# One row of reciprocal sums: two POOL transfers become one from ScalarE, and its transpose moves behind half a product

## The chip, the cores and the metric

The kernel runs on one core of a Trainium2 chip. The metric is the device time in microseconds of one execution. A core has a matrix engine (TensorE, in the profile PE, with its weight loads as PEld), a vector engine (VectorE, DVE), a scalar engine (ScalarE, ACT), GpSimd (POOL) and SyncE (SP), which here only issues transfers. Each engine works through its own list of instructions in order; semaphores tie the lists together. Transfers (DMAs) can be issued by SP, ACT and POOL, and all are carried out by the same 16 DMA engines.

## The reference

One layer with a state-space branch, an attention branch, a gated merge and an output projection, for 1024 positions and width 1024. What matters here is the attention, with 16 heads of width 64:

```python
fcum = jnp.cumsum(log_f, axis=-1)
for blk in range(seqlen // ATT_BLOCK):                       # blocks of 128 queries
    s = jnp.einsum('bhqd,bhkd->bhqk', q[:, :, q0:q1], k[:, :, :q1]) * scale
    s = s + fcum[:, :, q0:q1, None] - fcum[:, :, None, :q1]
    s = jnp.where(kpos[None, :] <= qpos[:, None], s, -jnp.inf)
    prob = jax.nn.softmax(s, axis=-1)
    outs.append(jnp.einsum('bhqk,bhkd->bhqd', prob, v[:, :, :q1]))
...
y_att = o * jax.nn.silu(z_att)
```

The softmax divides each query's weighted sum by the sum of its exponentials. In the kernel this division comes last: the weighted sum is formed without it, and is then multiplied by one over the sum. That reciprocal is the number whose way through the chip is changed here.

## The kernel before

**Stages.** The kernel has a prologue (norm, transposes), a state-space stage, an attention stage (about 669 to 1140 us of the profiled execution) and a tail with the last projections. Through all of them runs a `stream` of dense products for the projections, each split into a high and a low part and built as Strassen-like combinations of blocks. One step of the stream is a product of four 128-blocks by three part combinations, 12 matmuls of 128x128 by 512 columns; it is emitted as two halves of 6 matmuls (`Stream.half`), and after each half the stream may also emit loads, splits of operands and small chores. `fill(m, part)` emits as many halves as the plan gives to that place, so that TensorE has work while the attention's softmax passes through DVE and ACT.

**The attention loop.** Heads are worked in 8 pairs (`hp`), each pair in 6 visits (`g`), 48 visits `m = 6 hp + g` in all. A visit handles two blocks of 128 queries against one half (512) of the keys. Its parts, in the order in which they are emitted:

1. `scores`: four tiles of scores in PSUM (tag `s`, four banks); DVE adds the decay and takes the row minimum (line 1526, `ex`, `nm`), ACT takes the exponential with its row sum (line 1530, `ex`, `sm`).
2. `out` for the group of queries finished two visits ago: DVE multiplies by the reciprocals (`rb`, lines 1485 and 1491), and the outputs go on to DRAM from POOL (`ya_dram`, line 1581).
3. `weighted`: the weighted sums of the previous visit (`av`), with TensorE.
4. For the group finished in the previous visit: `free` (DVE, line 1479: weighted sum times gate, out of PSUM) and `send` (line 1446).
5. `settle` (the joint maximum of the two key halves), then `fill(m, 0)`.
6. `scale` (DVE: the reciprocals, tile `ns`, lines 1435 to 1444), loads for later visits on SP, `turned` (TensorE transposes the exponentials into PSUM tiles `pt`, DVE and ACT copy them out as `p`), and `take` (line 1456) for the group that was sent in this visit.
7. `fill(m, 1)`.

A group of queries ends with every second visit, three per pair of heads, 24 in all, and `send` and `take` run in the visits with even `m` after that.

**The row of reciprocals.** `ns` holds one number per query: 128 partitions (queries of a block) by 8 (two key halves or two block pairs `h`, two heads `e`, two blocks `t`). The outputs have the queries along the free axis, so the numbers must become a row and be spread over the 64 partitions of each head. `send` transposes `ns` with TensorE into a PSUM tile `tp` of 8 partitions by 128 (one of the four `s` banks), ACT copies it to a tile `st` (8x128, one of four buffers of the tag `th`, which the gates, the reloads and `rb` share), and POOL writes it to DRAM in two transfers, for `h = 0` and `h = 1`, so that DRAM holds it as `[e][h t c]`. `take` reads it back on SP into `rb`, 64 partitions times, one transfer for each head, 512 numbers in a row.

**What sets the order.** Instructions marked with `pin`, and all of TensorE's, stay in the order in which they are emitted. The others are put into each engine's list by a scheduler that simulates the program; `tc.high_priority()` puts an instruction ahead of the ones without it. The copy `st` has high priority; the POOL transfers are pinned.

Of the kernel before, what the change touches and what calls it, by code (L numbers as in the profile page):

```python
# [8 lines left out]
F32 = mybir.dt.float32  # L9
# [7 lines left out]
P = 128  # L17
T = 1024
D = 1024
NK = D // P  # L20
KH = NK // 2
NT = T // P
HALF = 512
# [63 lines left out]
def hybrid_layer(ctx: ExitStack, tc, a, out):  # L87

    nc = tc.nc
# [17 lines left out]
    nc.vector.memset(eps4, 4.0 * EPS)  # L107

    f_dram = tc.dram_tile([HEADS, T], F32, name="f_dram")
    st_dram = tc.dram_tile([NK, 3, 2, HALF], F32, name="st_dram")  # L110
    r_dram = tc.dram_tile([NG, T], F32, name="r_dram")
    rr_dram = tc.dram_tile([NG, T], F32, name="rr_dram")
    cs_dram = tc.dram_tile([HEADS, T], F32, name="cs_dram")
# [18 lines left out]
    def turn(out_, in_, idn=ident):  # L132
        return tc.keep_in_program_order(nc.tensor.transpose(out_, in_, idn))  # L133

    def pin(op):
        return tc.keep_in_program_order(op)

    def small(name="th"):
        return gp.tile([P, HALF], F32, tag="th", name=name)
# [185 lines left out]
    class Pair:  # L325
# [101 lines left out]
        def do(self, which):  # L427
            if which in (2, 4, 3) or which in (5, 7) and self.sums:
                unit, ch = {2: (0, 0), 4: (1, 0), 3: (0, 1)}.get(which, (1, 1))
                for begin in self.handlers[unit][2:]:  # L430
                    begin(ch)
            if which == 1:
                pool, tag = self.bank
                self.b = pool.tile([P, HALF], F32, tag=tag, bufs=1, name="pb")
                yield from self.matmuls(self.b, 1, "b11", True)
                self.k1 = self.keep(self.b)
            elif which == 2:
                pool, tag = self.other
                ps = pool.tile([P, HALF], F32, tag=tag, bufs=1, name="p" + tag)
                yield from self.matmuls(ps, 2, "b21", True)  # L440
                self.give(0, 0, ps, self.k1, "sum")
            elif which == 6:
                yield from self.matmuls(self.b, 6, "-t2", False)
                self.k2 = self.keep(self.b)
            elif which in (5, 7):
                if which == 5:
                    self.c = pj.tile([P, HALF], F32, tag="c", bufs=1, name="pc")
                    yield from self.matmuls(self.c, 5, "t1", True)
                else:
                    yield from self.matmuls(self.b, 7, "t3", False)  # L450
                    self.k7 = self.keep(self.b)
                self.sums += 1
                if self.sums == 2:
                    self.give(1, 1, self.c, self.k7, "less")
            elif which == 4:
                yield from self.matmuls(self.b, 4, "t4", False)
                (self.closing or (lambda ps: self.give(1, 0, ps)))(self.b)
            elif which == 3:
                yield from self.matmuls(self.c, 3, "-b22", False)
                self.give(0, 1, self.c, self.k2, "from")  # L460
# [26 lines left out]
    class Stream:  # L487
# [61 lines left out]
        def begin(self):  # L549
            self.load_next()  # L550
            self.load_next()
            for p, which in self.steps[:3]:
                self.prepare(p, which)
# [639 lines left out]
    with tc.tile_pool(name="pro", bufs=1, reuse_waits="tile", side="right") as pro, tc.tile_pool(  # L1193
        name="prop", bufs=1, space=PSUM, reuse_waits="tile", side="right"
# [6 lines left out]
        part = pro.tile([P, 1], F32, name="part")  # L1201
# [36 lines left out]
        def turned(tiles, k):  # L1238
            pt = prop.tile([P, HALF], F32, tag="pt", bufs=3, name="pt")
            for j in range(4):  # L1240
                turn(pt[:, j * P : (j + 1) * P], tiles[j][:, k * P : (k + 1) * P]) 
            return pt
# [10 lines left out]
        stream = Stream(order + late + ends, len(order) + 1, len(order) + len(late) + 4)  # L1253
# [57 lines left out]
    with tc.tile_pool(name="ssm", bufs=1, reuse_waits="tile", side="right") as sp, tc.tile_pool(  # L1311
        name="ssmp", bufs=1, space=PSUM, reuse_waits="tile", side="right"
# [42 lines left out]
    with tc.tile_pool(name="att", bufs=1, reuse_waits="tile", side="right") as ap, tc.tile_pool(  # L1355
        name="attp", bufs=1, space=PSUM, reuse_waits="tile", side="right"
    ) as pp:
        rows = [slice(64 * e, 64 * e + 64) for e in range(2)]
# [42 lines left out]
        class Heads:  # L1401
# [44 lines left out]
            def send(self, n):  # L1446

                tp = pp.tile([P, HALF], F32, tag="s", bufs=4, name="tp")
                turn(tp[0:8, 0:P], self.ns[n].rearrange("p h e t -> p (h e t)"))
                st = small("st")[0:8, 0:P]  # L1450
                with tc.high_priority():
                    nc.scalar.activation(st, tp[0:8, 0:P], AF.Copy)
                for h in range(2):
                    pin(nc.gpsimd.dma_start(st_dram[self.hp, n, :, 256 * h : 256 * h + 256], st[4 * h : 4 * h + 4, :]))

            def take(self, n):

                rb = self.rb[n] = small("rb")
                for e in range(2):
                    nc.sync.dma_start(rb[rows[e], :], st_dram[self.hp, n, e : e + 1, :].to_broadcast([64, HALF]))  # L1460

            def load_gates(self, n):

# [34 lines left out]
        def scores(hp, g, u):  # L1498

            pair, h = GROUPS[g]  # L1500
            i = pair[u]
            w = min(HALF, (i + 1) * P - h * HALF)
            s = [pp.tile([P, HALF], F32, tag="s", bufs=4, name="s") for e in range(2)]
            t, keys = q[hp, pair], k[hp, h]
            isl = slice(i % 2 * P, i % 2 * P + P)
            ops = [(t[:, x, isl], keys[:, y, 0:w]) for x, y in ((0, 0), (0, 1), (1, 0))]
            diagonal = h == i // 4
            for m, (x, y) in enumerate(ops):
                for e in range(2):
                    mm(  # L1510
                        s[e][:, 0:w], x[rows[e]], y[rows[e]], start=(m == 0), stop=(m == 2 and not diagonal),
                        skip_group_check=True,
                    )
            if diagonal:
                for n, (x, y) in enumerate(corner):
                    for e in range(2):
                        mm(
                            s[e][:, w - P : w], x[rows[e]], y[rows[e]], start=False, stop=(n == 1),
                            skip_group_check=True,
                        )  # L1520
            hd = heads[hp]
            for e in range(2):
                o = ex[:, e, u, 0:w]
                nm = hd.at(hd.nm, i, h, e)
                pin(
                    nc.vector.tensor_tensor_reduce(  # L1526
                        o, s[e][:, 0:w], fb[hp, h][:, e, 0:w], 1.0, 3.0e38, ALU.add, ALU.min, nm
                    )
                )
                pin(nc.scalar.activation(o, o, AF.Exp, scale=-1.0, bias=nm, accum_out=hd.at(hd.sm, i, h, e)))  # L1530
# [108 lines left out]
        def end(m):  # L1639

            hp, g = divmod(m, 6)
            if 0 <= hp < NK and g % 2:
                yield heads[hp], g // 2
# [12 lines left out]
        rooms = [(0.8, 0.35), (0.8, 0.35), (0.55, 0.25), (0.8, 0.35), (0.75, 0.35), (0.5, 0.25)]  # L1656
        left = [sum(map(sum, rooms)) * sum(weights)]

        def fill(m, part):
            share = weights[min(m // 6, NK - 1)] * rooms[m % 6][part]  # L1660
            to = stream.steps.index((ends[4], 6))
            stream.halves(round((2 * (to - stream.at) - (stream.run is not None)) * share / left[0]))
            left[0] -= share

        made = []
        for m in range(6 * NK + 1):

            stream.visit = m + 1
            hp, g = divmod(m, 6)
            if not g and hp < NK:  # L1670
                heads[hp] = Heads(hp)
            if m < 6 * NK:
                for u in range(2):
                    scores(hp, g, u)
            for hd, which in end(m - 2):
                hd.out(which)
            for one in made:
                weighted(*one)
            for hd, which in end(m - 1):
                hd.free(which)  # L1680
                if m < 6 * NK:
                    hd.send(which)
            stream.release()
            if m == 6 * NK:
                heads[NK - 1].out(2)
                stream.visit = 0
                break
            for hd, which in end(m):
                hd.settle(which)
            fill(m, 0)  # L1690

            for hd, which in end(m):
                hd.scale(which)
                hd.load_gates(which)
            loads(m)
            made = turned(hp, g)
            for hd, which in end(m - 1):
                hd.take(which)
            if m == 6 * NK - 1:
                heads[hp].send(2)  # L1700
            stream.hold()
            fill(m, 1)
            if m == 6 * NK - 1:
                heads[hp].take(2)
# [59 lines left out]
```

## Time and profile before

| | |
|---|---|
| three runs | 1291.77, 1297.4 and 1297.5 us, median 1297.4 us |
| profiled execution, its own time | 1294.79 us |
| its span in the trace | 1293.1 us (1.7 us lie around it) |
| granted TensorE clock | 0.997 |
| busy share of the span | PE 97%, DVE 78%, ACT 61%, POOL 22% |
| sends | 24 transposes `tp`, 24 copies `st`, 48 POOL transfers, 48 SP reads `rb` |

A row of a group reads: line, engine, operation, output<-inputs, shapes, count, then busy time in us, mean ns of one, then the engine's idle time just before these instructions and what ended it. In the timeline a row is start, duration, engine, line, operation, and in brackets the idle time before it. `SPq`, `ACTq` mean the engine's list of issues, not the transfer itself; the time "to landing" runs from the issue to the semaphore that tells of its end.

### The profile page before, as it was taken

The page shows a single profiled execution, that of the slowest core. Times are in us where ns is not written, and L with a number is a line of the kernel's source. Part 1 is how long each engine was busy: PE and PEld are TensorE (multiplying, and loading weights), DVE is VectorE, ACT ScalarE, POOL GpSimd, SP SyncE. Part 2 cuts the span into 40 slices and gives each one's busy share as a digit, 9 for nine tenths or more (in the row PEclk, how much of TensorE's full clock was granted, in tenths as well). Part 3 has the DMA queues.
Part 4 walks back from the last instruction along what each step waited for, and adds up shares of the span by engine and source line. Part 5 has one row for each costly group of instructions (what it writes and reads, how often), then busy time and mean ns, then how long its engine had stood idle before and what let it go on. Part 6 is the DMA issues. An engine that isn't in the chain of part 4 may idle for free. (4 is left out here: it accounts for less than half of the span.)

```text
span 1293.1 us, 21078 instructions
## 1 busy us (share of the span) xinstructions
PE 1253.8 (97%) x7066; PEld 986.1 (76%) x7066; DVE 1014.7 (78%) x1979; ACT 794.3 (61%) x1728; POOL 284.6 (22%) x307
## 2 busy tenths in 40 slices
PE   6999999999999999899999999999999999999998
PEld 4787888788888888688776777777767777678786
DVE  6998888888789878788676766676789767876875
ACT  8755666466556756566555666566677556743654
POOL 0000330024102320143001222222121313256052
PEclk9999999999999999999999999999999999999999
DMA  7332543644363545445564657666677657665932
GB/s 281 104 106 71 154 148 121 199 140 146 127 210 116 153 153 164 122 154 154 168 237 153 221 175 224 193 208 196 228 282 250 219 178 253 230 219 189 364 112 102
DMA packets 154669, 233.60 MB, mean 181 GB/s; under 512 B 17216, under 2 KB 62656, under 8 KB 154560
## 3 DMA queue, kind: packets, MB, share of 16 engines
q1 hardware_dynamic: 142016, 205.53, 49.8%
q0 software_dynamic: 6400, 16.10, 3.3%
q10 hardware_dynamic: 6144, 10.62, 2.2%
q8 instruction: 56, 0.92, 0.3%
q14 instruction: 53, 0.43, 0.1%
HBM read 162.99 MB, written 72.34 MB: 182 GB/s over the span
## 5 line engine op out<-in xcount | busy, mean ns | idle before, releaser
L356 DVE TENSOR_TENSOR wop<-sum,wop 128x512 fp32r<-128x512 f32 x174 | 140.5, 808 | 53.4 <-ACT wop L354 52.7
L354 ACT ACTIVATE wop<-sum 128x512 fp32r<-128x512 f32 x174 | 108.8, 626 | 99.0 <-DVE sum L363 44.7
L1530 ACT ACTIVATE ex<-ex,nm 128x512 f32<-128x512 f32 (+1 forms) x192 | 116.1, 606 | 76.9 <-DVE nm L1526 75.7
L410 ACT ACTIVATE s<-pb 128x512 f32<-128x512 f32 x141 | 83.5, 592 | 97.3 <-PE pb L130 95.9
L130 PE MATMUL pc<-x3h,wop 128*128 128x512 f32 x384 | 131.6, 399 | 2.5 <-ACT wop L354 2.0
L130 PE MATMUL pb<-x0h,wop 128*128 128x512 f32 x384 | 132.2, 400 | 0.7 <-ACT x0h L1246 0.6
L130 PE MATMUL pc<-x2h,wop 128*128 128x512 f32 x384 | 131.4, 399 | 0.4 <-DVE u L422 0.4
L130 PE MATMUL pb<-x6h,wop 128*128 128x512 f32 x376 | 129.2, 399 | 1.6 <-ACT s L410 1.6
L130 PE MATMUL pb<-x5h,wop 128*128 128x512 f32 x376 | 128.3, 398 | 1.3 <-ACT s L410 1.3
L130 PE MATMUL pb<-x4h,wop 128*128 128x512 f32 x376 | 128.6, 398 | 0.2 <-DVE wop L356 0.2
L356 DVE TENSOR_TENSOR wop<-raw,wop 128x512 fp32r<-128x512 f32 x149 | 104.3, 702 | 29.8 <-ACT wop L354 29.5
L1526 DVE CUSTOM_DVE_ANT_0 ex<-s,fb 128x512 f32<-128x512 f32 (+1 forms) x192 | 96.8, 553 | 24.4 <-PE s L130 24.3
L354 ACT ACTIVATE wop<-raw 128x512 fp32r<-128x512 f32 x151 | 93.8, 623 | 15.8 <-PE pc L130 10.1
L130 PE MATMUL pd<-x1h,wop 128*128 128x512 f32 x264 | 89.1, 396 | 0.0
L130 PEld LDWEIGHTS pc<-x3h,wop 128*128 128x128 f32 x384 | 72.1, 188 | 20.2 <-issue 3.8
L130 PEld LDWEIGHTS pb<-x0h,wop 128*128 128x128 f32 x384 | 72.5, 189 | 17.2 <-ACT x0h L1246 1.3
L130 PEld LDWEIGHTS pc<-x2h,wop 128*128 128x128 f32 x384 | 72.1, 188 | 16.1 <-DVE u L422 0.8
L130 PEld LDWEIGHTS pb<-x6h,wop 128*128 128x128 f32 x376 | 70.6, 188 | 18.1 <-ACT s L410 2.7
L130 PEld LDWEIGHTS pb<-x5h,wop 128*128 128x128 f32 x376 | 70.6, 188 | 17.5 <-ACT s L410 2.2
L130 PEld LDWEIGHTS pb<-x4h,wop 128*128 128x128 f32 x376 | 70.5, 188 | 15.7 <-issue 0.7
L130 PE MATMUL s<-k,q 64*128 64x512 f32 (+3 forms) x576 | 75.7, 373 | 6.2 <-DVE p L1548 4.4
L214 POOL TENSOR_TENSOR wd<-wd 128x256 f32<-128x256 f32 x32 | 31.3, 978 | 228.3 <-DMA wd<-in_wo 125.7
(341 smaller groups left out, 3012.1 us busy)
## 6 DMA issues: line engine op xcount, KB each, us to landing
raw<-in_wu SPq DMA_DIRECT2D x128, 256.0 KB, 3.7
csb<-cs_dram SPq DMA_DIRECT2D x32, 256.0 KB, 5.5
fb<-f_dram SPq DMA_DIRECT2D x16, 512.0 KB, 6.5
rb<-st_dram SPq DMA_DIRECT2D x48, 128.0 KB, 3.2
wd<-in_wo SPq DMA_DIRECT2D x40, 128.0 KB, 3.1
xt<-in_x SPq DMA_DIRECT2D x8, 512.0 KB, 5.8
gs_dram<-th ACTq DMA_DIRECT2D x16, 256.0 KB, 3.4
qh_dram<-th SPq DMA_DIRECT2D x16, 256.0 KB, 5.2
```

What stands on the lines that cost most here:

```text
L130: return tc.keep_in_program_order(nc.tensor.matmul(*args, **kw))
L214: pin(nc.gpsimd.tensor_tensor(t[out_], t[a_], t[b_], ALU.subtract))
L354: nc.scalar.activation(op[:, 0], src, AF.Copy, scale=sign)
L356: nc.vector.tensor_tensor(op[:, 1], src, op[:, 0], ALU.subtract)
L410: nc.scalar.activation(s, ps, AF.Copy)
L1526: nc.vector.tensor_tensor_reduce(o, s[e][:, 0:w], fb[hp, h][:, e, 0:w], 1.0, 3.0e38, ALU.add, ALU.min, nm)
L1530: pin(nc.scalar.activation(o, o, AF.Exp, scale=-1.0, bias=nm, accum_out=hd.at(hd.sm, i, h, e)))
```

## The change

Four edits that belong together:

- The scratch tensor in DRAM gets the shape of the tile that is stored, `[8, 128]` for each send. The rows lie as `(h e t)` in place of `(e)(h t)`.
- `send` stores the tile with one transfer, issued from ACT's list behind the copy, with the copy's priority and no pin. POOL issues none.
- `take` reads for each head two pieces of 256 numbers in place of one of 512, still one transfer for each head to 64 partitions.
- The loop no longer calls `send` behind `free`. `fill` gets a list of things to do behind its first half: it emits one half of a product, calls `send` for the group of the previous visit, and emits the rest. The number of halves is the same. The last send, at the end of the loop, stays where it was.

```diff
-    st_dram = tc.dram_tile([NK, 3, 2, HALF], F32, name="st_dram")
+    st_dram = tc.dram_tile([NK, 3, 8, P], F32, name="st_dram")
...
                 with tc.high_priority():
                     nc.scalar.activation(st, tp[0:8, 0:P], AF.Copy)
-                for h in range(2):
-                    pin(nc.gpsimd.dma_start(st_dram[self.hp, n, :, 256 * h : 256 * h + 256], st[4 * h : 4 * h + 4, :]))
+                    nc.scalar.dma_start(st_dram[self.hp, n], st)
...
                 rb = self.rb[n] = small("rb")
+                by_head = st_dram[self.hp, n].rearrange("(h e t) c -> e h (t c)", h=2, e=2)
                 for e in range(2):
-                    nc.sync.dma_start(rb[rows[e], :], st_dram[self.hp, n, e : e + 1, :].to_broadcast([64, HALF]))
+                    to = rb[rows[e], :].rearrange("p (h c) -> p h c", h=2)
+                    nc.sync.dma_start(to, by_head[e : e + 1].to_broadcast([64, 2, 256]))
...
-        def fill(m, part):
+        def fill(m, part, behind=()):
             share = weights[min(m // 6, NK - 1)] * rooms[m % 6][part]
             to = stream.steps.index((ends[4], 6))
-            stream.halves(round((2 * (to - stream.at) - (stream.run is not None)) * share / left[0]))
+            n = round((2 * (to - stream.at) - (stream.run is not None)) * share / left[0])
             left[0] -= share
+            stream.halves(min(n, 1))
+            for do in behind:
+                do()
+            stream.halves(max(n - 1, 0))
...
             for hd, which in end(m - 1):
                 hd.free(which)
-                if m < 6 * NK:
-                    hd.send(which)
             stream.release()
...
-            fill(m, 0)
+            fill(m, 0, [lambda hd=hd, which=which: hd.send(which) for hd, which in end(m - 1)])
```

## The prediction

> **What bounds the kernel now.** First the page, for the busiest engine and its clock; then the same shares for the stretch in which the sends run; then what TensorE waits for inside it.
>
> ```profile
> span 1293.1 us, 21078 instructions
> ...
> PE 1253.8 (97%) x7066; PEld 986.1 (76%) x7066; DVE 1014.7 (78%) x1979; ACT 794.3 (61%) x1728; POOL 284.6 (22%) x307
> ```
>
> ```profile
> 687.00:1140.00 453.00, 441.71 (x2972) 334.04 (x2966) 335.66 (x831) 292.64 (x728) 104.12 (x140) 1.00 0.66 217
> ```
>
> The second row is the attention stage: 453.00 us, of them PE 441.71, then PEld, DVE 335.66, ACT 292.64 and POOL 104.12; granted clock 1.00; the DMA engines 0.66 busy. TensorE sets the time. It is idle for 453.00 - 441.71 = 11.3 us here, and no edit that leaves its work as it is can win more than that, apart from stalls that the modelled ends of its matmuls hide. The idle time by group, in the same window:
>
> ```profile
> L130 PE MATMUL s<-k,q 64*128 64x512 f32 (+2 forms) x540 | 71.3, 374 | 6.2 <-DVE p L1548 4.4 <-ACT p L1550 1.6
> L133 PE MATMUL pt<-ident,ex 128*128 128x128 f32 x546 | 67.8, 273 | 1.6 <-ACT ex L1530 1.5
> L133 PE MATMUL tp<-ident,ns 128*8 128x128 f32 x24 | 6.5, 273 | 2.6 <-DVE nm L1526 1.5 <-DVE ns L1444 1.1
> L133 PEld LDWEIGHTS tp<-ident,ns 128*8 128x8 f32 x24 | 2.0, 83 | 10.3 <-DVE nm L1526 7.6 <-issue 2.6
> ```
>
> The last column is idle time before the group. The transposes `tp` that the change moves have 2.6 us of matmul idle and 10.3 us of load idle before them. The timeline says which of the two counts:
>
> ```profile
> 686.85 0.60 PE L130 MATMUL av<-p,v 128*64 128x256 f32 x4
> ...
> 687.38 0.08 PEld L133 LDWEIGHTS tp<-ident,ns 128*8 128x8 f32 x1 [0.38 <-DVE nm L1526]
> 687.38 0.27 PE L133 MATMUL tp<-ident,ns 128*8 128x128 f32 x1
> ...
> 687.41 0.48 PE L130 MATMUL pb<-x5h,wop 128*128 128x512 f32 x1
> ...
> 688.81 0.25 ACT L1452 ACTIVATE st<-tp 8x128 f32<-8x128 f32 x1
> ...
> 689.36 1.30 POOL L1454 DMA_DIRECT2D st_dram<-st  x2 [7.59 <-ACT st L1452]
> ```
>
> ```profile
> 957.24 0.39 PE L130 MATMUL av<-p,v 128*64 128x128 f32 x4
> ...
> 958.86 0.08 PEld L133 LDWEIGHTS tp<-ident,ns 128*8 128x8 f32 x1 [1.48 <-DVE nm L1526]
> 958.86 0.27 PE L133 MATMUL tp<-ident,ns 128*8 128x128 f32 x1 [1.24 <-DVE nm L1526]
> ...
> 960.93 0.25 ACT L1452 ACTIVATE st<-tp 8x128 f32<-8x128 f32 x1
> ```
>
> ```profile
> 1002.45 0.27 PE L133 MATMUL tp<-ident,ns 128*8 128x128 f32 x1 [1.09 <-DVE ns L1444]
> ...
> 1003.08 0.25 ACT L1452 ACTIVATE st<-tp 8x128 f32<-8x128 f32 x1
> ```
>
> At 687.38 the load has 0.38 us of idle and the matmul none: the weighted sums ran until 687.45, so the array was still at work. The idle of the loads is mostly that. Real waits stand at 958.86 (1.24 us, the PSUM bank that the transpose takes is still being read by DVE at line 1526) and 1002.45 (1.09 us, DVE came late to `ns`): 2.33 of the 2.6 us. The change can remove 2.6 us here, not 10.3.
>
> **The change part by part.**
>
> *The transpose behind half a product.* A whole step of the stream is 12 matmuls, as this row of the chain shows:
>
> ```profile
> 1146.26 2.72 PE pd L130 x12
> ```
>
> So half a step is 1.36 us of cover, more than either of the two waits (1.24 and 1.09); both should go, and with them the 2.6 us. Where the stall goes: TensorE reaches its next scores earlier by as much and may wait there for `p` (the 6.2 us row), so I take 2.0 of 2.6 as kept, with 0 and 2.6 as ends. The transpose itself costs the same between two products as between `av` and a product: the next product starts 0.03 us behind it at 687.41, its first matmul lasts 0.48 us. If the new place hides none of it, it is at most 24 x 0.273 = 6.5 us; I take 0, since that row already shows a product behind it.
>
> *The copy and the row's departure.* The copy `st` starts not when `tp` is done but when ACT gets through its four exponentials: 1.43, 2.07 and 0.63 us behind `tp` in the three cuts above. With `tp` 1.36 us later, less the wait that goes (0, 1.24, 1.09), and 0.27 us of transpose, `st` would start 0.2 us later in the first and not later in the other two. Over all sends the bounds are 0 and 1.36 us; I take 0.5, nearer to these cuts than to the far end, since sends with a shorter lag than theirs are not excluded. Before, POOL needs two issues behind `st`:
>
> ```profile
> L1454 POOL DMA_DIRECT2D st_dram<-st x48: 549/577/736, 689.4 to 1136.6; - x48
> L1452 ACT ACTIVATE st<-tp x24: 250/251/268, 688.8 to 1135.5; 8x128 f32<-8x128 f32 x24
> ...
> DMA to landing us min/median/max: 1.6/3.0/6.3
> ```
>
> The first starts 689.36 - 688.81 = 0.55 us behind the copy's start, the second 0.58 later: 1.13 us. From ACT's own list the issue can start when the copy ends, at 0.25. The row thus leaves 1.13 - 0.25 - 0.5 = 0.4 us earlier. How long it then takes, the trace shows only for larger stores of ACT:
>
> ```profile
> L654 ACTq DMA_DIRECT2D ga_dram<-th x16: 326/326/360, 839.1 to 981.1; - x16
> ...
> DMA to landing us min/median/max: 2.0/3.7/6.6
> ```
>
> Between 1.6 and 6.6 us, as wide as POOL's 1.6 to 6.3. Long landings belong to moments when SP has just issued a large load: at 689.36 the landing was the slow kind, and the decay row for the next heads, 512 KB, had been issued at 688.46.
>
> ```profile
> 688.46 0.41 SPq L1395 DMA_DIRECT2D fb<-f_dram  x1
> ...
> 696.28 1.13 SPq L1460 DMA_DIRECT2D rb<-st_dram  x2
> ...
> 700.55 0.69 DVE L1491 TENSOR_TENSOR o<-o,rb 128x512 f32<-128x512 f32 x1 [4.37 <-DMA rb<-st_dram]
> ...
> 705.52 1.65 PE L130 MATMUL s<-k,q 64*128 64x512 f32 x6 [3.21 <-DVE p L1548]
> ```
>
> I take the landing time as unchanged. [...]
>
> *Reading the row back.* Each read now has 1 KB pieces. The trace has reads of the same 128 KB in 1 KB pieces, those of the queries:
>
> ```profile
> rb<-st_dram SPq DMA_DIRECT2D x48, 128.0 KB, 3.2
> ...
> q<-qh_dram SPq DMA_DIRECT2D x29, 128.0 KB, 3.8
> ```
>
> That bounds the loss at 0.6 us per read and 0 below; I take 0.3. Together with the 0.4 us gained, `rb` arrives within a few tenths of when it did. Who waits for it:
>
> ```profile
> SPq L1460 <- DMA st_dram<-st: 87.6, 21, 7.3
> ```
>
> ```profile
> DVE o L1491 <- DMA rb<-st_dram: 11.7, 8, 4.4
> ```
>
> SP stands at the read for 87.6 us in 21 sends, with the loads of later weights and queries behind it; no row of TensorE's idle time names such a load. DVE waits 11.7 us in 8 sends, and the cut above shows one of them reaching TensorE: 4.37 us of DVE at 700.55 became 3.21 us of PE at 705.52. Both stay, at 0 us of change.
>
> *ACT issues, POOL doesn't.* POOL is relieved of 48 x 0.577 = 27.7 us; it is busy for 104 of 453 us, and its list stands waiting for the row 163.5 us, so it has room: 0.
>
> ```profile
> POOL st_dram L1454 <- ACT st L1452: 163.5, 24, 17.4
> ```
>
> ACT gets 24 issues:
>
> ```profile
> 802.93 0.34 ACTq L654 DMA_DIRECT2D gs_dram<-th  x1
> ...
> 803.31 1.57 ACT L1550 ACTIVATE p<-pt 128x512 f32<-128x512 f32 x3 [0.41 <-ACT th L653]
> ```
>
> An issue holds ACT for 0.41 us, 24 x 0.41 = 9.8 us. Queued behind it are a split of weights, `s` and the copies `p`, for which TensorE's next scores wait. What hides it: ACT is idle for 453 - 292.64 = 160 us, and stands before the copies waiting for the transposes:
>
> ```profile
> ACT p L1550 <- PE pt L133: 13.2, 29, 1.2
> ```
>
> 29 of its copies find ACT early. I take 0 to TensorE; without the cover it is 9.8 us.
>
> *The scratch layout, the buffer.* One 4 KB store in place of two of 2 KB: nothing beside the landing. `st` takes its `th` buffer one half later in the rotation and gives it back sooner; unknown, bounded by the one wait of a read for another store's buffer in this trace, a few us of SP, either sign; 0.
>
> Sum: -2.0 + 0 + 0 + 0 = -2.0 us. The profiled execution took 1294.79 us, so 1292.8 for it; that execution lies 2.6 us below the median of the three runs (1297.4), which would become 1295.4. I predict 1294, between the two.
>
> **The rivals.**
>
> *Even (the forecast):* 1290 to 1298. For it: PE at 97%, and only 2.6 us of idle at the place that is changed.
>
> *The row gets past SP's loads.* If ACT's queue lands the row in the shortest 1.6 us where POOL's took 6.3, DVE's wait of 4.37 us at 700.55 goes, with it the 3.21 us of PE at 705.52 and some of the slow scores behind (1.65 us for six). 2.6 + 3.2 + about 1.5 = 7.3 us less: 1287.5 from the profiled time. Against it: ACT's other stores land no faster than POOL's.
>
> *ACT becomes the gate (slower).* Copy and issue sit in ACT's list, in order, behind a transpose that TensorE now does later. If they come directly ahead of the copies `p`, less than 0.25 + 0.41 = 0.66 us before the transposes are done, each send delays the next scores by its 0.41 us: +9.8 - 2.6 = +7.2, 1302. It decides where only one half is left between `tp` and the transposes. At 687.38 the two were 2.9 us apart (two halves), so after the move 1.5 us: enough there, hence the low chance. That the list is reordered elsewhere by the scheduler comes under the same price.
>
> *The wait only moves.* `tp` no longer waits but the following scores do, by the same 2.6 us: 1294.8 as before.
>
> **How the numbers follow.** Even 0.55, the wait only moves 0.07, the row gets past 0.22, ACT the gate 0.16. What a measurement of this kernel can tell is about 0.5%, 6.5 us. The second rival is beyond that bound and takes another 0.05 from the lower edge of the forecast: faster 0.27; slower 0.16; same 0.57. The likeliest case alone spans 1290 to 1298; to hold 8 in 10 the range reaches to 1286 and 1301.
>
> **What would show it.** Idle before `tp` near 0 in the matmul row, while the load's idle moves to the first product behind `av`. `st` some 0.5 us later against the scores, POOL's group gone, an ACT issue of 0.33 us with landings again from 1.6 to over 5. DVE's wait for `rb` near 12 us: at 4 the first rival holds, at 25 the row comes later than I say. Scores waiting for ACT's `p` at clearly more than 1.6 us show the slower rival. I am wrong if PE's idle time in the stage leaves 7 to 13 us.

## The result, and the profile after

The changed kernel takes 1302.2 us (median of 9 runs, 1299.35 to 1307.0); the kernel before takes 1295.17 us (median of 9 runs beside them). The ratio is 1.006, with a 95% interval of 1.0046 to 1.0074: 7 us, 0.6% slower. The profiled executions differ by as much, 1301.84 against 1294.79 us.

The page's head, and the attention stage with its groups on TensorE (columns as in the rows of before):

```profile
span 1300.1 us, 20959 instructions
...
PE 1260.3 (97%) x7066; PEld 988.7 (76%) x7066; DVE 1019.0 (78%) x1979; ACT 794.5 (61%) x1728; POOL 255.6 (20%) x259
```

```profile
687.00:1140.00 453.00, 440.23 (x2952) 330.84 (x2948) 334.62 (x827) 290.04 (x723) 72.20 (x89) 1.00 0.65 214
```

```profile
L130 PE MATMUL s<-k,q 64*128 64x512 f32 (+2 forms) x540 | 70.3, 368 | 5.9 <-ACT p L1551 3.2 <-DVE p L1549 2.1
L133 PE MATMUL pt<-ident,ex 128*128 128x128 f32 x546 | 68.4, 273 | 1.8 <-ACT ex L1531 1.1 <-ACT st L1452 0.7
L130 PE MATMUL pc<-x3h,wop 128*128 128x512 f32 x103 | 37.1, 409 | 3.2 <-ACT x3h L281 3.2
L133 PE MATMUL tp<-ident,ns 128*8 128x128 f32 x24 | 6.5, 272 | 1.7 <-DVE ns L1444 1.5
```

The averages look as forecast. TensorE idles 453.00 - 440.23 = 12.8 us in the stage, against 11.3. ACT is not busier (290.04 against 292.64) and POOL is relieved (72.20 against 104.12). Three things are new: a wait of 3.2 us for `x3h`, which had none, `p` from ACT with 3.2 in place of 1.6 us, and 0.7 us of `pt` for the copy `st`. The window also holds 20 matmuls fewer (2952 against 2972), so the stage is behind by its end in a way that its idle time doesn't tell.

**Where the time goes.** TensorE executes the same 7066 matmuls, and all but the moved transposes `tp` in the same order, so the start of each of these in one trace can be set against the start of the same one in the other. The difference, after minus before, in us:

```
at (time of after)   after - before
start of attention        +0.4
708                       -3.2     first stall for rb shorter
955                       -3.6     wait of tp at 958.86 gone
961                       -3.1     tp itself, now at its new place
968                       -0.5     lost around send 14
1087                      +2.6     small pieces, each under 1 us
1130                      +1.6
1139                      +5.2     standstill for x3h
1146                      +7.5     slow matmuls behind it
end                       +7.1
```

The change wins 4 us by 955 and loses nearly 11 after it, most of it at two places. (The sends count from 0 to 23.)

**First place: send 22, the last but one.** Before, from the timeline around it:

```profile
1117.25 1.95 PE L130 MATMUL av<-p,v 128*64 128x256 f32 x16
...
1119.13 0.27 PE L133 MATMUL tp<-ident,ns 128*8 128x128 f32 x1
...
1120.21 0.25 ACT L1452 ACTIVATE st<-tp 8x128 f32<-8x128 f32 x1
...
1121.84 1.14 ACT L281 ACTIVATE x5h<-x5l 128x512 fp32r<-128x512 f32 x2
...
1123.43 1.09 SPq L1460 DMA_DIRECT2D rb<-st_dram  x2
```

The same send after:

```profile
1119.26 1.95 PE L130 MATMUL av<-p,v 128*64 128x256 f32 x16
...
1122.63 0.27 PE L133 MATMUL tp<-ident,ns 128*8 128x128 f32 x1
...
1124.45 1.14 ACT L281 ACTIVATE x5h<-x5l 128x512 fp32r<-128x512 f32 x2
1125.49 0.25 ACT L1452 ACTIVATE st<-tp 8x128 f32<-8x128 f32 x1
...
1125.77 0.27 ACTq L1453 DMA_DIRECT2D st_dram<-st  x1
...
1128.80 1.24 SPq L1461 DMA_DIRECT2D rb<-st_dram  x2
```

Counted from the start of `av`, `tp` starts 1.5 us later (3.37 against 1.88), and `st` 2.86 instead of 1.08 us behind `tp`. Two splits `x5h` now stand ahead of the copy in ACT's list (1.04 us of the 1.78), and it comes behind all four exponentials of the visit, where before it stood behind two. SP's read is 3.4 us later (9.54 against 6.18). What hangs on that row is the end of the attention. Before:

```profile
1128.53 0.69 DVE L1491 TENSOR_TENSOR o<-o,rb 128x512 f32<-128x512 f32 x1
...
1130.52 0.63 ACT L278 ACTIVATE x4h<-x 128x512 fp32r<-128x512 f32 x1 [0.84 <-DVE x L1593]
...
1133.46 0.62 ACT L281 ACTIVATE x3h<-x3l 128x512 fp32r<-128x512 f32 x1
```

After:

```profile
1133.10 0.69 DVE L1492 TENSOR_TENSOR o<-o,rb 128x512 f32<-128x512 f32 x1 [1.99 <-DMA rb<-st_dram]
...
1135.01 0.63 ACT L278 ACTIVATE x4h<-x 128x512 fp32r<-128x512 f32 x1 [2.77 <-DVE x L1594]
...
1137.06 0.62 ACT L354 ACTIVATE wop<-raw 128x512 fp32r<-128x512 f32 x1
...
1138.10 0.62 ACT L278 ACTIVATE x2h<-zr 128x512 fp32r<-128x512 f32 x1
1138.62 0.61 ACT L281 ACTIVATE x3h<-x3l 128x512 fp32r<-128x512 f32 x1
...
1139.29 0.50 PE L130 MATMUL pc<-x3h,wop 128*128 128x512 f32 x1 [3.20 <-ACT x3h L281]
```

DVE's `o` is 4.57 us later, ACT's `x4h` (made from it) 4.49, `x3h` 5.16. `x3h` itself needs nothing of this row: the loads of its inputs were issued by 1114.4. It lies in ACT's list behind splits that do need the row (`x4h` waits 2.77 us for DVE), and TensorE's next instruction needs `x3h`.

**Behind the standstill the clock is lower.** Windows of after (stretch, its length, busy PE, PEld, DVE, ACT and POOL, granted clock, DMA share, GB/s):

```profile
1136.00:1139.00 3.00, 0.09 (x1) 0.00 (x0) 2.59 (x6) 3.00 (x7) 0.54 (x1) 1.00 0.35 137
1139.00:1142.00 3.00, 2.23 (x7) 1.08 (x9) 2.42 (x5) 2.49 (x6) 0.00 (x0) 0.64 0.04 8
1142.00:1146.00 4.00, 4.00 (x15) 2.87 (x12) 2.98 (x5) 0.68 (x2) 0.00 (x0) 0.50 0.51 156
```

Some 6 us at half the clock turn the lag of 5.2 us into 7.5. Before has the same thing behind its own standstill of 3.21 us at 705.52:

```profile
705.00:708.00 3.00, 2.48 (x16) 1.83 (x16) 1.62 (x3) 0.63 (x2) 0.00 (x0) 0.59 0.23 87
```

After, that first stall is 1.09 us and the clock stays at 1.00; this is the early gain:

```profile
703.86 0.96 PE L130 MATMUL s<-k,q 64*128 64x512 f32 x6 [1.09 <-DVE p L1549]
```

**Second place: send 14.** The timeline of after:

```profile
957.09 0.27 PE L133 MATMUL tp<-ident,ns 128*8 128x128 f32 x1
...
961.84 0.25 ACT L1452 ACTIVATE st<-tp 8x128 f32<-8x128 f32 x1
...
962.14 0.44 PE L133 MATMUL pt<-ident,ex 128*128 128x128 f32 x2 [0.69 <-ACT st L1452]
...
962.51 0.61 ACT L653 ACTIVATE th<-th 128x512 f32<-128x512 f32 x1
963.90 0.29 ACTq L1453 DMA_DIRECT2D st_dram<-st  x1
964.24 0.60 ACT L410 ACTIVATE s<-pb 128x512 f32<-128x512 f32 x1 [1.11 <-DMA x5l<-t_s]
965.25 0.59 ACT L1551 ACTIVATE p<-pt 128x512 f32<-128x512 f32 x1
...
965.89 0.97 PE L130 MATMUL s<-k,q 64*128 64x512 f32 x6 [1.92 <-ACT p L1551]
```

The wait of `tp` (1.24 us before) is gone, but `st` starts 4.75 us behind it, the transposes `pt` now wait for the PSUM bank that `st` reads, and the scores wait 1.92 us for `p`. ACT stands from the end of `th` at 963.12 until the issue at 963.90. Both waits together are 2.6 us, the whole loss between 961 and 968.

### The profile page after: what moved, and what is told of

It is laid out like the page before. It is cut to its first block, busy times and chain, and to the rows that moved or that the text cites. A ratio compares the mean times of both kernels' runs of the same rounds, so it can differ in the third digit from the quotient of the medians.

```text
span 1300.1 us, 20959 instructions
## 1 busy us (share of the span) xinstructions
PE 1260.3 (97%) x7066; PEld 988.7 (76%) x7066; DVE 1019.0 (78%) x1979; ACT 794.5 (61%) x1728; POOL 255.6 (20%) x259
## 4 chain that ended last, share of the span: by engine, by line
PE 67%; DVE 12%; DMA 11%; ACT 5%; issue 3%; SPq 1%; POOL 0%; ACTq 0%; DVEq 0%; POOLq 0%
PE pb L130 29%; PE pc L130 16%; PE pd L130 5%; PE av L130 4%; PE s L130 4%; PE pt L133 3%; PE yps L130 2%; DVE wop L356 2%; DMA raw<-in_wu 1%; PE tr L133 1%; DMA qh_dram<-th 1%; DVE sum L363 1%; DMA st_dram<-st 1%; PE st L130 1%; ACT ex L1531 1%
## 5 line engine op out<-in xcount | busy, mean ns | idle before, releaser
L130 PE MATMUL pc<-x3l,wop 128*128 128x512 f32 x192 | 76.0, 396 | 0.5 <-DVE x3l L282 0.5
```

Of the source, the lines that this page charges most:

```text
L130: return tc.keep_in_program_order(nc.tensor.matmul(*args, **kw))
```

## The experiments

The theory after reading the two traces: the new place delays single rows (P in the expectations of the first runs), and two of them are where it shows. The rivals: ACT's issue costs, the new layout of the scratch and of the reads costs, or the low clock is all of it. Ratios are to the kernel before on the same chip, each with its 95% interval. Diffs are against the changed kernel, unless another is named.

**1. The place alone.** The layout of before with its two POOL transfers, at the new place:

```diff
-                    nc.scalar.dma_start(st_dram[self.hp, n], st)
+                for h in range(2):
+                    pin(nc.gpsimd.dma_start(st_dram[self.hp, n, :, 256 * h : 256 * h + 256], st[4 * h : 4 * h + 4, :]))
```

> The send moves behind the first half product, but POOL still stores the row with two transfers and the row keeps its old layout. Theory P (the place is at fault: the copy falls behind operand splits in ScalarE's list, the row of single sends comes late, and DVE's wait for it reaches TensorE): slower than before by at least as much as the whole change, 1302 to 1307, since POOL's way is 0.85 us longer. Theory T (the transfer in ScalarE's list is at fault): no slower than before, 1292 to 1296. Theory S (any new order of the list moves the time, no part by itself): anywhere within 1290 to 1303, without a relation to the row's lateness.

Measured: 1315.08 us, ratio 1.0155 (1.0129 to 1.0182), 20 us slower and more than either theory said. The place is costly. But its profiled execution was 4.9 us behind before the attention began, where the lists are the same as before, so not all of its loss can be put down to the sends. Most of the 4.9 us arises in the windows of 240 to 260 and 525 to 550 us, whose granted clock is 0.91 and 0.93 (before 1.00 in both). The trace of run 5 is 4.0 us behind by 550 us, with a median no slower than before: so such a loss also comes without the new place.

**2. The transfer alone.** ACT's transfer and the new layout, `send` at its old place:

```diff
-            fill(m, 0, [lambda hd=hd, which=which: hd.send(which) for hd, which in end(m - 1)])
+            fill(m, 0)
...
             for hd, which in end(m - 1):
                 hd.free(which)
+                if m < 6 * NK:
+                    hd.send(which)
```

> One transfer from ScalarE and the new layout, but the send stays behind the weighted sums. Theory P: faster than before by 3 to 7 us (1288 to 1292), since the row leaves 0.85 us earlier and TensorE's wait at the first row (3.2 us and the slow scores behind it) goes. Theory T: slower, 1300 or more, TensorE waiting for ScalarE's copies p. Theory S: anywhere within 1290 to 1303.

Measured: 1300.25 us, 1.0035 (1.0017 to 1.0053): slower, where P had it faster by 3 to 7 us. So the transfer is no gain that the place spoils; it has a cost of its own. ACT's timeline shows it, at one send out of 24 (send 15):

```profile
982.90 0.25 ACT L1452 ACTIVATE st<-tp 8x128 f32<-8x128 f32 x1
985.64 0.29 ACTq L1453 DMA_DIRECT2D st_dram<-st  x1
985.98 1.15 ACT L281 ACTIVATE x6h<-x6l 128x512 fp32r<-128x512 f32 x2 [2.83 <-DMA x2l<-ys_dram]
...
990.12 0.58 ACT L1551 ACTIVATE p<-pt 128x512 f32<-128x512 f32 x1
```

The copy ends at 983.15, the issue starts at 985.64. The bracket names a load of SP, `x2l<-ys_dram`; the last of its issues is at 977.50, eight issues of SP and ACT ahead of this one. What such a pair shares, the traces of before and of the change show: the issues of SP and ACT carry the same eight completion semaphores (100, 102 to 107 and 109), 845 of 908 before and 832 of 932 in the change the one of the issue eight earlier, and POOL's carry eight others. In the change send 14 has the semaphore of the load `x5l` that was issued at 955.19, eight issues earlier; that load lands at 963.82, and the issue starts at 963.90. Send 15 there has that of the same `x2l` as here, issued at 977.24 and landed at 984.81, and starts at 984.88. So I take the stand in run 2 as one for the load, on a semaphore that the two share. ACT's whole list stands meanwhile: from `st` to `p` it needs 7.22 us, against 4.29 in the kernel before (983.31 to 987.60).

**3. The change, but the last pair of heads sends at the old place.**

```diff
+                if hd.last and m < 6 * NK:
+                    hd.send(which)
...
-            fill(m, 0, [... for hd, which in end(m - 1)])
+            fill(m, 0, [... for hd, which in end(m - 1) if not hd.last])
```

> The whole change, but the sends of the last pair of heads (two of the 24) stay behind the weighted sums. Theory P: the wait of 3.2 us for the split x3h at the end of the attention, with 2.4 us of slow products behind it, goes: 5 to 6 us less than the whole change, 1296 to 1297. Theory T: at most 0.5 us less, since 22 of 24 sends are as in the change. Theory S: no clear sign.

Measured: 1301.09 us, 1.0043 (1.0026 to 1.0059): 1.1 us better than the change, with intervals that overlap, and not 5 to 6. The wait for `x3h` falls from 3.20 to 1.15 us, but behind it stands a new one, and then the low clock again. The timeline and the windows of this run:

```profile
1147.56 0.50 PE L130 MATMUL pb<-x5h,wop 128*128 128x512 f32 x1 [2.74 <-ACT s L410]
```

```profile
1150.00:1154.00 4.00, 4.00 (x14) 3.16 (x13) 2.57 (x5) 1.12 (x2) 0.50 (x2) 0.69 0.66 207
```

ACT's list has `x1h<-zr`, a split of the last outputs, ahead of the `s` that TensorE needs. The wait moved to the next row that the end of the attention hangs on.

**4. The change, with TensorE kept busy in the standstill.** 14 needless products behind the last send:

```diff
                 heads[hp].send(2)
+                warmer = pp.tile([P, HALF], F32, tag="s", bufs=4, name="warmer")
+                for n in range(14):
+                    mm(warmer, k[hp, 0][:, 0, 0:P], k[hp, 0][:, 0, :], start=n == 0, stop=n == 13)
```

> The whole change, with 14 needless products of 128 by 512 behind the last send (3.2 us of TensorE's time), where TensorE otherwise stands still for 3.2 us. It computes the same. If the products behind the standstill are slow because TensorE stood still (granted clock 0.50 and 0.64 there): the products behind run at 0.227 us again and the time is 2 to 2.4 us less than the change, about 1300. If they are slow for another reason (operands, transfers): the same time as the change or up to 1 us more, 1302 to 1303.

Measured: 1300.48 us, 1.0038 (1.0023 to 1.0054), 1.7 us less than the change, with intervals that overlap. The products fill the standstill and the clock stays up:

```profile
1133.58 3.47 PE L130 MATMUL warmer<-k 128*128 128x512 f32 x14
```

```profile
1134.00:1138.00 4.00, 3.99 (x18) 2.90 (x16) 3.58 (x8) 4.00 (x9) 0.54 (x1) 1.00 0.35 124
1138.00:1142.00 4.00, 3.53 (x19) 2.31 (x19) 3.50 (x7) 2.51 (x6) 0.00 (x0) 1.00 0.16 51
```

The idle time is gone in this run, and the low clock with it. In four other traces a standstill of 3.2 us has it behind it: before 0.59 (705 to 708 us), the change 0.64 and 0.50 (1139 to 1146), run 6 0.59 and 0.55 (1142 to 1150), run 9 0.50 (1138 to 1142). Its price is less sure: in the trace of the change the lag grew by 2.35 us, the medians say 1.7, and the added products also made the scheduler put an `s` ahead of `x1h<-zr` in ACT's list.

**5. The new layout, with one transfer from POOL, at the old place.** The kernel of run 2, with

```diff
-                    nc.scalar.dma_start(st_dram[self.hp, n], st)
+                pin(nc.gpsimd.dma_start(st_dram[self.hp, n], st))
```

> The send at its old place, the new layout, one transfer, but issued by POOL. Theory L (ScalarE's list stands at the issue until the transfer eight places earlier on the shared hardware completion semaphores has landed, as for 2.5 us at 985.64 of the transfer-only kernel): ScalarE never stands at an issue, the row leaves 0.58 us earlier than before: no slower than before, 1291 to 1296. Theory R (the new layout, with 1 KB pieces and reads that hold SP's list 0.60 in place of 0.45 us, is at fault): about 1300, as with the transfer from ScalarE.

Measured: 1293.42 us, 0.9992 (0.9976 to 1.0008): no difference. The layout, the reads in 1 KB pieces and one transfer for two are harmless.

**6. The change, with that same POOL transfer.**

> The whole change, but its one transfer is issued by POOL. Theory L: the stop of 1.8 us at 963.90 of the changed kernel goes, while the row of every send leaves 0.3 us later than with ScalarE, which the end of the attention pays: 1299 to 1303. Theory R: 1302 as the change. If the place alone makes the 20 us of the place-only kernel, and not the second issue of POOL, it would be near 1310.

Measured: 1308.75 us, 1.0118 (1.0093 to 1.0142). The place costs 15.3 us with POOL's single transfer, against run 5. The waits of its TensorE (engine, what waits, for what: us in all, times, longest) carry the same wait for `x3h`, and a long one for `p`, 5.03 us, behind send 21, whose row SP reads 12.9 us behind the start of `av`'s last matmul (5.7 before):

```profile
PE s L130 <- DVE p L1549: 8.8, 5, 5.0
PE pc L130 <- ACT x3h L281: 3.2, 1, 3.2
```

**7. ACT's transfer at the old place, but send 15 from POOL.** The kernel of run 2, with

```diff
-                    nc.scalar.dma_start(st_dram[self.hp, n], st)
+                    if (self.hp, n) != (5, 0):
+                        nc.scalar.dma_start(st_dram[self.hp, n], st)
+                if (self.hp, n) == (5, 0):
+                    pin(nc.gpsimd.dma_start(st_dram[self.hp, n], st))
```

> The transfer-only kernel, with one of its 24 transfers (send 15, the one before which ScalarE stood for 2.5 us) issued by POOL. Theory L: that stop and the 3.5 to 4 us that TensorE loses behind it go: 1296 to 1297, against 1300.25. Theory R: as the transfer-only kernel, 1299 to 1301.

Measured: 1294.73 us, 1.0004 (0.9987 to 1.0021). One issue out of 24 taken from ACT gives 5.5 us back by the medians and 4 by the ratios (the trace of run 2 lost 4.4 us at this send), and ACT's list is as quick as before there, 4.28 us from `st` to `p`:

```profile
985.69 0.25 ACT L1452 ACTIVATE st<-tp 8x128 f32<-8x128 f32 x1
...
989.97 0.57 ACT L1554 ACTIVATE p<-pt 128x512 f32<-128x512 f32 x1
```

So the cost of ACT's transfer at the old place is, within some 2 us, that one stand.

**8. The change, but send 14 from POOL.** The edit of run 7, with `(4, 2)`, in the changed kernel:

> The whole change, with one of its 24 transfers (send 14, before which ScalarE stood for 1.8 us) issued by POOL. Theory L: about 3 us less than the change, 1299. Theory R: no difference, 1302.

Measured: 1302.05 us, 1.0062 (1.0042 to 1.0081): nothing gained, where 1299 was expected. The 1.8 us of the expectation count from the end of the copy and hold a split and `th` as well; ACT stands for 0.78 us. By the starts of the matmuls this trace loses 1.8 us at the spot, the change 2.6, and run 6, which has no issue on ACT, 1.5, with the same wait of `pt` for `st`. So the stand is about 0.8 us of it, too little for the medians to show, and the larger part is the place: the copy comes behind four splits in ACT's list and holds its PSUM bank.

**9. Run 5, with send 22 alone moved.**

```diff
             for hd, which in end(m - 1):
                 hd.free(which)
+                if m < 6 * NK and (hd.hp, which) != (7, 1):
+                    hd.send(which)
...
-            fill(m, 0, [... for hd, which in end(m - 1)])
+            fill(m, 0, [... for hd, which in end(m - 1) if (hd.hp, which) == (7, 1)])
```

> One transfer from POOL, and of the 24 sends only send 22 (the second group of the last pair of heads, the last but one of all) stands behind the half product. Theory E (the end of the attention pays for the place: row late, DVE late, the splits behind it in ScalarE's list late, TensorE still for 3.2 us and slow for some 4 us behind it): 4 to 6 us more than the same kernel with all sends at the old place (1293.4), so 1297 to 1300. Theory M (each moved send costs its part, 15 us over 23 sends with POOL): 0.7 us more, 1294.

Measured: 1297.51 us, 1.0026 (1.0012 to 1.0040), 4.1 us above run 5. One moved send brings the whole end: the splits ahead of the copy, a wait of 3.21 us for `x3h`, and the clock. Its timeline and the window behind that wait:

```profile
1121.40 1.14 ACT L281 ACTIVATE x5h<-x5l 128x512 fp32r<-128x512 f32 x2
1122.44 0.25 ACT L1452 ACTIVATE st<-tp 8x128 f32<-8x128 f32 x1
```

```profile
1138.00:1142.00 4.00, 4.00 (x14) 2.36 (x14) 3.09 (x6) 1.42 (x3) 0.05 (x1) 0.50 0.02 5
```

**10. Run 5, with the first twelve sends moved** (the same edit, with `hd.hp < KH`, the first four pairs of heads).

> One transfer from POOL, and the 12 sends of the first four pairs of heads stand behind the half product, the others at the old place. Theory E: no cost, 1292 to 1295. Theory M: 12 of 23 parts of 15 us, about 8 us more than 1293.4, so 1301.

Measured: 1292.92 us, 0.9996 (0.9984 to 1.0008): the place costs nothing there.

**11. The whole change for the first twelve sends, run 5 for the others** (run 10, with ACT's transfer where `self.hp < KH`).

> The whole change for the 12 sends of the first four pairs of heads (place and transfer from ScalarE), the others at the old place with one transfer from POOL. Theory E: what the change gains until 955 us of its execution (2.3 us, TensorE's wait at 705 us) is kept and nothing is paid later: 1290 to 1293, ahead of both kernels. Theory M: 4 us more than 1295 (half of the change's 7): 1299.

Measured: 1291.78 us, 0.9981 (0.9970 to 0.9992). It is the lowest median of all, 0.2% below the kernel before and 10.4 us below the change; its interval overlaps those of runs 5, 10 and 12, so these four cannot be ranked. DVE's waits for the row, by its profile, are shorter than before too (11.7 us then), as they are in run 10, where POOL has the transfer:

```profile
DVE o L1495 <- DMA rb<-st_dram: 7.2, 6, 2.1
```

**12. The transfer from SP, at the old place** (run 5, with `nc.sync.dma_start(st_dram[self.hp, n], st)`).

> All sends at the old place, one transfer, issued by SP, whose list stands at the read of that row anyway. If the transfer from ScalarE costs only because ScalarE's list stands at the issue: no such stop here, as with POOL, 1291 to 1296. If a shared hardware semaphore's wait costs wherever it stands: about 1300. SP's loads behind the store leave later than with POOL, up to 1 us per send, which could cost as much as the row gains.

Measured: 1293.34 us, 0.9988 (0.9971 to 1.0005): as from POOL, no difference to the kernel before.

The runs as a table of medians in us; the kernels before on the three chips lie between 1294.8 and 1295.4:

| transfer | old place | new place |
|---|---|---|
| two from POOL, old layout | 1295.17 (before) | 1315.08 (run 1) |
| one from POOL | 1293.42 (run 5) | 1308.75 (run 6) |
| one from ACT | 1300.25 (run 2) | 1302.20 (the change) |
| one from SP | 1293.34 (run 12) | not tried |

The two halves of the change don't add. The place costs 15 us with POOL's transfer and 2 us with ACT's; ACT's transfer costs 7 us at the old place, and saves 6.5 at the new one. The 2 us are no more than a hint, since the intervals of run 2 and the change overlap. That ACT's transfer saves at the new place because a late row leaves without POOL's delay is argued, not shown.

## Why the prediction was wrong

It said 1294 us, no difference, with a range up to 1301. The time is 1302.2. By its own steps:

**The waits of `tp`: right in kind.** It took 2.0 of 2.6 us as won. The 1.24 us at 958.86 are gone; the other did not go but is now 1.5 us for the same `ns`, since DVE came later too. Left are 1.7 us, so 0.9 was won.

**The copy, "0.5 us later, bounds 0 and 1.36": the step that failed.** Counted from the start of `av`'s last matmul, the copy is 1.6 us later on the mean of the 24 sends (3.37 against 1.73), and more than 1.36 later at 14 of the 23 that moved. On the mean the shorter way behind the copy makes up for that: SP's read comes 6.28 us behind that matmul, before 6.38. Single sends are far outside the bounds. At send 22 `st` is 3.3 us later against `av` (6.23 instead of 2.96 us behind its start). The bound rested on ACT's list keeping its order, so that only the half product counts. But ACT's list is made by the scheduler, which put two splits and two more exponentials ahead of `st`. Those are ACT's own work, not a wait, and no lag seen in the old list could bound them. The sum has 0 for this; send 22 alone costs 4.1 us (run 9).

**"Both stay, at 0 us of change": failed by reading sums.** DVE's waits for `rb` in the stage were 14.8 us before (11.7 for `o`, 3.1 for `zr`) and are 11.0 now, near the 12 that the prediction named. After, the rows are

```profile
DVE o L1492 <- DMA rb<-st_dram: 10.0, 7, 2.2
DVE zr L1486 <- DMA rb<-st_dram: 1.0, 2, 0.5
```

It is not how long DVE waits but at which row. 1.99 of these us stand at 1133.10, at the head of a chain through DVE, ACT's splits and `x3h`, at whose end TensorE stands still for 3.20 us. Run 9 shows that this one place is 4.1 us. In the first half twelve moved sends cost nothing (run 10).

**ACT's issues, "hidden, 0": right for 23 of 24.** They take 0.29 us and are covered; all but send 14's start within 0.11 us of the copy's end in the change. The price was set by their duration, which was the wrong quantity: two issues also stood until a load of SP eight issues earlier had landed. That was 0.78 us at send 14, of which run 8 shows nothing in the median; at the old place 2.49 us at send 15, worth 4 to 5.5 (run 7).

**Layout, reads, buffer, POOL, at +0.3 and 0: right** (run 5).

**The clock: not in the sum.** The row at 705.52 was quoted with its six scores in 1.65 us, and the first rival priced them; that the same could follow other standstills was not carried over to losses. Behind the change's 3.20 us (clock 0.64 and 0.50) it is about 2 us.

**The rivals.** "The row gets past SP's loads" came true in part: the stall at 705.52 fell from 3.21 to 1.09 us, and the kernel was 3.2 us ahead at 708. That is the change's gain, and run 11 has 2.1 us of it without the losses. But ACT's queue alone does not bring it: with ACT's transfer at the old place (runs 2 and 7) the stall is still 2.8 to 2.9 us, with POOL's one transfer 2.1 there (run 5), and 1.7 at the new place (run 10). From the store's issue to SP's read of this first row it took 6.9 us before (689.36 to 696.28) and 4.1 in the change (690.08 to 694.14). Why is not shown. "ACT becomes the gate" gave 1302, the time that came, by another way: not 24 small delays of 0.41 us but two places. Its sign, scores waiting clearly over 1.6 us for `p`, is there (3.2), of which 1.92 at send 14.

**Its test of itself** was blunt: PE's idle time in the stage is 12.8 us, inside the 7 to 13 that were to hold if it was right. A fixed window takes slow matmuls as busy time, and the work that has left the window isn't seen.

**The account of the loss.** Run 11 is 10.4 us faster than the change, so that is what the second twelve sends cost. Run 9, with POOL's transfer, puts 4.1 of it on send 22, the traces 2.6 on send 14. The other 3.7 us (the trace has 3.1 in small pieces between 968 and 1087) have no cause that a run shows.

## What to carry to other kernels

Price a moved step at each of its instances, not by the mean lag: look for the instance with which a stage ends, follow what it releases through the in-order lists, and ask whether TensorE still has independent work there. When a scheduler makes an engine's list, a small move elsewhere can put whole splits ahead of the copy that matters, and high priority did not prevent it here. A change that is good in one part of a loop and bad in another is best tried on half of the loop (1291.78 against 1302.2 us).

## What was not expected of the hardware

**Behind some standstills of two or three us TensorE's granted clock was 0.50.** Idle times of 3.2 us were followed by stretches at a granted clock of 0.50 to 0.64 in the change and in run 9, and 2.74 us by 0.69 in run 3. Shorter ones were followed too, such as 2.02 us at 705.70 in run 11:

```profile
707.70:709.70 2.00, 2.00 (x14) 1.11 (x12) 1.39 (x6) 2.00 (x7) 0.00 (x0) 0.50 0.43 129
```

So was one of 1.96 us, at 535.22 in the change. The windows 535.66 to 539.07 and 539.07 to 541 there:

```profile
535.66:539.07 3.41, 3.41 (x10) 2.62 (x9) 3.41 (x7) 2.95 (x8) 0.00 (x0) 0.50 0.39 120
539.07:541.00 1.93, 1.93 (x9) 1.57 (x9) 1.05 (x3) 1.71 (x4) 0.00 (x0) 1.00 1.05 261
```

But the same wait in the kernel before, 1.99 us at 535.21, was followed by a clock of 1.00, as were 2.51 us at 543.54 there and 1.92 us at 965.89 in the change: in these traces the length alone does not decide below 3.2 us. A stretch at 0.50 lasted 3.41 us (before, from 705.54; the change, from 535.66) or 6.83 us (the change, from 1139.82). In run 4, where products fill the standstill, the clock stayed at 1.00.

**ACT's list stood at its own transfer until a load of SP had landed.** At send 15 of run 2 it stood 2.49 us; the load had been issued 8.1 us earlier (977.50 against 985.64). The kernel took 1300.25 us with the transfer from ACT (run 2) and 1293.42 with it from POOL (run 5), at the same place. At send 14 of the change it stood 0.78 us, until 963.90; the load had landed at 963.82.
